# Three of the four weight sums of each pair made by accumulating transfers that GpSimd issues, in place of VectorE additions

## The chip, the cores and the metric

The kernel is one program on one core of a Trainium2 chip. The metric is the time of one execution on the device, in microseconds (us). Engines are named as in the profile: PE is TensorE's matmul side, DVE is VectorE, ACT is ScalarE, POOL is GpSimd, SP is SyncE, which here only issues transfers. A trailing q (SPq) is an engine's sequencer.

## The reference

One transformer block on 512 tokens of width 1024: a feed-forward part, a mixer of two attentions, and a second feed-forward part. Only the feed-forward parts matter here:

```python
def rmsnorm(x, g):
    xf = x.astype(jnp.float32)
    y = xf * lax.rsqrt(jnp.mean(xf * xf, axis=-1, keepdims=True) + RMS_EPS)
    return (y * g.astype(jnp.float32)).astype(x.dtype)

def swiglu(h, w_gate, w_up, w_down):
    return (jax.nn.silu(h @ w_gate) * (h @ w_up)) @ w_down

def reference(x, ...):
    x = x + 0.5 * swiglu(rmsnorm(x, norm_ffn1[l]), w_ffn1_gate[l], w_ffn1_up[l], w_ffn1_down[l])
    x = x + hybrid_mixer(rmsnorm(x, norm_mix[l]), ...)
    x = x + 0.5 * swiglu(rmsnorm(x, norm_ffn2[l]), w_ffn2_gate[l], w_ffn2_up[l], w_ffn2_down[l])
    return rmsnorm(x, norm_final)
```

The width of the feed-forward part is 2816. Everything is float32.

## The kernel before

**Feed-forward blocks.** There are two, both of the class Ffn; I call them block 1 and block 2. The 2816 hidden features are taken in 22 columns of 128. The first 4 are made plainly (`plain`), the other 18 in 9 pairs (`pair`). A pair computes gate (m = 0) and up (m = 1) for two columns with a scheme that needs 7 block products where the plain way needs 8 (the Strassen-Winograd scheme): weights are cut into A11, A12, A21, A22 (first index: which of the two columns; second: which half of the 1024 inputs), the input into B blocks, and the products take A11, A12, A22 and four sums of weights, S1 to S4. Each sum overwrites a weight tile: S1 goes to A21 (A21 + A22), S2 to A11 (A11 + S1), S3 to A21 again (S2 - A22), S4 to A12 (A12 + S2). So S2 needs S1; S3 and S4 need S2.

**Precision.** Each float32 weight block is split into a high half (ACT, line 236, tile sph) and the remainder (DVE, line 237, tile spl), and PE multiplies in three passes (lines 101 to 103, high by high, high by low, low by high). One block product is a step of 12 matmuls of 256 columns. The tiles of halves have 6 buffers each; the weight tiles (aw) have 16, the 8 of one pair twice.

**Order.** `go` walks a list of steps, each with up to five parts: load, sum, halves, products, and what is done with the result. Loads are recorded 12 steps ahead of the products, sums 6, halves 4. Between the steps of a pair stand steps of the down projection (`down`), whose weights come in 512 KB pieces (tile raw, 4 buffers), are split on ACT (line 92, tile whi) and DVE (line 96, wlo), and are multiplied in matmuls of 512 columns. The scheduler of the language then orders each engine's instructions by the times that it reckons with; an engine runs its own in order. All weights are fetched by SP, one after the other in a fixed order (`fetch`); a fetch waits until the tile that it overwrites is free, and all fetches behind it wait too.

**GpSimd** helps in the attention and at the very end; in the feed-forward pairs it does nothing.

The products of a block's first pair overlap with the last down steps of the plain columns.

Of the kernel before, what the change touches and what calls it, by code (L numbers as in the profile page):

```python
# [12 lines left out]
ALU = mybir.AluOpType  # L13
AX = mybir.AxisListType

S = 512
# [13 lines left out]
def block_kernel(ctx: ExitStack, tc: tile.TileContext, A: dict, out: bass.AP):  # L30
# [7 lines left out]
    nc = tc.nc  # L38
# [78 lines left out]
    for k in range(NK):  # L117
        x = xp.tile([128, S], F32, name=f"x{k}")
# [73 lines left out]
    class Ffn:  # L192
# [114 lines left out]
        def pair(self, f):  # L307
# [3 lines left out]
            def loads(m, j):  # L311
                for i in range(2):
                    A[m, i, j] = self.sp.tile([128, 4, 128], F32, name="aw", tag="aw", bufs=16)
                    fetch(A[m, i, j], self.w[m][f + i][:, 4 * j:4 * j + 4])

            def sums(m, name):

                a11, a12, a21, a22 = [A[m, i, j] for i in range(2) for j in range(2)]
                to, x, y, op = {"S1": (a21, a21, a22, ALU.add), "S2": (a11, a21, a11, ALU.add),
                                "S3": (a21, a11, a22, ALU.subtract), "S4": (a12, a11, a12, ALU.add)}[name]  # L320
                with self.behind_lo():
                    nc.vector.tensor_tensor(to, x, y, op)  # L322

            def halves_of(m, name):
                i, j = {"A11": (0, 0), "A12": (0, 1), "S1": (1, 0), "S2": (0, 0), "S3": (1, 0), "S4": (0, 1),
                        "A22": (1, 1)}[name]
                hi = self.sp.tile([128, 4, 128], F32R, name="sph", tag="sph", bufs=6)
                lo = self.sp.tile([128, 4, 128], F32R, name="spl", tag="spl", bufs=6)
                self.halves_of_x(hi, lo, A[m, i, j])
                half[m, name] = hi, lo  # L330

            def run(m, to, a, b, first):
                if first:
                    bank[m, to] = ps.tile([128, S], F32, name="p" + to, tag={"u": "s", "v": "t", "w": "o"}[to],
                                          bufs=2)[:, :HT]
                hi, lo = half.pop((m, a))
                for k, x in enumerate(self.moving(b)):
                    self.in_pair = mm3(bank[m, to], (hi[:, k], lo[:, k]), x, first and k == 0, k == 3, not first)
                    if k == 1:
                        self.between(self.held == 0 and len(self.waiting) > 4)  # L340
                self.between(self.held == 0)
                self.held = max(self.held - 1, 0)

            def copied(m, to, name):
                part[m, name] = self.sp.tile([128, HT], F32, name="wc", tag="wc", bufs=4)
                nc.scalar.activation(part[m, name], bank[m, to], AF.Copy)  # L346
# [29 lines left out]
            for n, (to, a, b, first, then) in enumerate((  # L376
                    ("u", "A11", "B11", True, lambda m: copied(m, "u", "u1")),
                    ("v", "A12", "B21", True, c11),
                    ("w", "S1", "T1", True, lambda m: copied(m, "w", "w1")),
                    ("u", "S2", "T2", False, lambda m: copied(m, "u", "u2")),  # L380
                    ("u", "S3", "T3", False, c22),
                    ("w", "S4", "B22", False, c12),
                    ("u", "A22", "T4", False, c21))):
                for m in range(2):
                    steps.append([(lambda m=m, n=n: loads(m, n)) if n < 2 else None,
                                  (lambda m=m, a=a: sums(m, a)) if a[0] == "S" else None,
                                  lambda m=m, a=a: halves_of(m, a),
                                  lambda m=m, to=to, a=a, b=b, first=first: run(m, to, a, b, first),
                                  lambda m=m, then=then: then(m)])
# [75 lines left out]
        def go(self, after):  # L465
            steps, at = self.steps, [0, 0, 0]
            late, count = None, 0
            for i, s in enumerate(steps):
                for j, ahead in enumerate((12, 6, 4)):
                    while at[j] < min(i + ahead + 1, len(steps)):  # L470
                        if steps[at[j]][j]:
                            steps[at[j]][j]()
                        at[j] += 1
                down = len(s) == 6
                if down and late:
                    late()
                s[3]()
                if not down:
                    if late:
                        late()  # L480
                    if i == 2 * FP - 1:
                        s[4]()
                        s[4] = None
                    after(count)
                    count += 1
                late = s[4]
            if late:
                late()
            self.between(len(self.waiting))
# [757 lines left out]
```

## Time and profile before

| | |
|---|---|
| median of 3 runs | 992.03 us (991.65 to 992.7) |
| profiled execution | 990.21 us, its span 988.4 |
| granted TensorE clock | 0.997 of full speed |
| PE busy | 970.5 us, 98% of the span |
| DVE busy | 778.5 us, 79% |
| ACT busy | 561.9 us, 57% |
| POOL busy | 132.5 us, 13% |
| weight sums on DVE (line 322) | 144 |

How to read the views. A busy time is the union of an engine's instructions. Matmuls are pipelined: a row of one lasts longer than the distance to the next start, so PE can lose a tenth of a microsecond between two matmuls and still be shown busy. In a timeline the square bracket holds the engine's idle time before an instruction and what ended it. A table of stretches gives each engine's busy time in a stretch, the number of instructions, the granted clock, DMA's busy share and the rate that it moved. For transfers, the time from issue to landing is given as a median.

### The profile page before, as it was taken

The page shows a single profiled execution, that of the slowest core. Times are in us where ns is not written, and L with a number is a line of the kernel's source. Part 1 is how long each engine was busy: PE and PEld are TensorE (multiplying, and loading weights), DVE is VectorE, ACT ScalarE, POOL GpSimd, SP SyncE. Part 2 cuts the span into 40 slices and gives each one's busy share as a digit, 9 for nine tenths or more (in the row PEclk, how much of TensorE's full clock was granted, in tenths as well). Part 3 has the DMA queues.
Part 4 walks back from the last instruction along what each step waited for, and adds up shares of the span by engine and source line. Part 5 has one row for each costly group of instructions (what it writes and reads, how often), then busy time and mean ns, then how long its engine had stood idle before and what let it go on. Part 6 is the DMA issues. An engine that isn't in the chain of part 4 may idle for free.

```text
span 988.4 us, 16902 instructions
## 1 busy us (share of the span) xinstructions
PE 970.5 (98%) x6084; PEld 859.0 (87%) x6084; DVE 778.5 (79%) x1579; ACT 561.9 (57%) x1165; POOL 132.5 (13%) x176
## 2 busy tenths in 40 slices
PE   9999999999999999999999999999999999999996
PEld 7789999999999898787878888888999999999985
DVE  6996997688776587768788978789898788777744
ACT  6464655445544366567677886655475445454435
POOL 0000000000000000035666676100000000000002
PEclk9999999999999999999999999999999999999998
DMA  7255534332321125531121232226254322341102
GB/s 257 97 185 173 196 129 133 110 102 91 97 68 43 58 88 190 181 113 33 53 72 43 87 85 80 71 86 213 67 166 153 119 73 95 101 128 44 54 11 86
DMA packets 50056, 104.52 MB, mean 106 GB/s; under 512 B 10129, under 2 KB 14690, under 8 KB 49972
## 3 DMA queue, kind: packets, MB, share of 16 engines
q1 hardware_dynamic: 49684, 102.91, 32.4%
q8 instruction: 48, 0.79, 0.3%
q10 hardware_dynamic: 288, 0.52, 0.1%
q14 instruction: 36, 0.29, 0.1%
HBM read 97.98 MB, written 5.30 MB: 104 GB/s over the span
## 4 chain that ended last, share of the span: by engine, by line
PE 91%; DVE 4%; issue 1%; ACT 1%; DMA 1%; POOL 0%; SPq 0%; POOLq 0%; ACTq 0%; DVEq 0%
PE pd L102 8%; PE pd L103 8%; PE pd L101 8%; PE pu L101 6%; PE pu L103 6%; PE pu L102 6%; PE pw L101 4%; PE pw L103 4%; PE pw L102 4%; PE pp L103 3%; PE pp L101 3%; PE pp L102 3%; PE pgu L102 3%; PE pgu L101 3%; PE pgu L103 3%; PE ps_t L940 3%
## 5 line engine op out<-in xcount | busy, mean ns | idle before, releaser
L236 ACT ACTIVATE sph<-aw 128x512 fp32r<-128x512 f32 x252 | 157.3, 630 | 197.4 <-PE pu L102 71.1
L237 DVE TENSOR_TENSOR spl<-aw,sph 128x512 fp32r<-128x512 f32 x252 | 172.3, 690 | 59.7 <-ACT sph L236 57.2
L92 ACT ACTIVATE whi<-raw 128x512 fp32r<-128x512 f32 (+1 forms) x200 | 121.5, 619 | 126.4 <-PE pd L102 44.2
L102 PE MATMUL pd<-h,whi 128*128 128x512 f32 x336 | 132.7, 395 | 0.0
L103 PE MATMUL pd<-h,wlo 128*128 128x512 f32 x336 | 131.1, 393 | 0.0
L96 DVE TENSOR_TENSOR wlo<-raw,whi 128x512 fp32r<-128x512 f32 (+1 forms) x168 | 111.7, 676 | 24.1 <-ACT whi L92 20.6
L101 PE MATMUL pd<-h,whi 128*128 128x512 f32 x336 | 130.4, 394 | 0.0
L101 PE MATMUL pu<-th,sph 128*128 128x256 f32 x432 | 119.4, 276 | 0.3 <-ACT wc L346 0.3
L103 PE MATMUL pu<-th,spl 128*128 128x256 f32 x432 | 119.4, 276 | 0.0
L102 PE MATMUL pu<-tl,sph 128*128 128x256 f32 x432 | 119.2, 276 | 0.0
L322 DVE TENSOR_TENSOR aw<-aw 128x512 f32<-128x512 f32 x144 | 99.0, 689 | 0.0
L531 DVE SCALAR_TENSOR_TENSOR x<-pd,x 128x512 f32<-128x512 f32 x88 | 60.1, 689 | 33.3 <-PE pd L103 33.3
L101 PEld LDWEIGHTS pu<-th,sph 128*128 128x128 f32 x432 | 81.1, 188 | 4.6 <-ACT wc L346 0.5
L102 PEld LDWEIGHTS pu<-tl,sph 128*128 128x128 f32 x432 | 81.1, 188 | 4.0
L103 PEld LDWEIGHTS pu<-th,spl 128*128 128x128 f32 x432 | 81.1, 188 | 0.1
L101 PE MATMUL pw<-xo,sph 128*128 128x256 f32 x288 | 79.7, 277 | 0.2 <-ACT sph L236 0.2
L102 PE MATMUL pw<-xo,sph 128*128 128x256 f32 x288 | 79.5, 276 | 0.0
L103 PE MATMUL pw<-xo,spl 128*128 128x256 f32 x288 | 79.4, 277 | 0.0
L103 PEld LDWEIGHTS pd<-h,wlo 128*128 128x128 f32 x336 | 63.1, 188 | 13.8
L102 PEld LDWEIGHTS pd<-h,whi 128*128 128x128 f32 x336 | 63.1, 188 | 4.0
L101 PEld LDWEIGHTS pd<-h,whi 128*128 128x128 f32 x336 | 63.1, 188 | 3.7
L101 PEld LDWEIGHTS pw<-xo,sph 128*128 128x128 f32 x288 | 54.1, 188 | 3.9 <-ACT sph L236 0.6
(246 smaller groups left out, 2443.1 us busy)
## 6 DMA issues: line engine op xcount, KB each, us to landing
aw<-in_wg SPq DMA_DIRECT2D x72, 256.0 KB, 2.8
aw<-in_wu SPq DMA_DIRECT2D x72, 256.0 KB, 4.5
raw<-in_wd1a SPq DMA_DIRECT2D x20, 512.0 KB, 3.9
raw<-in_wd2a SPq DMA_DIRECT2D x20, 512.0 KB, 4.8
raw<-in_w_a SPq DMA_DIRECT2D x16, 512.0 KB, 4.8
raw<-in_w SPq DMA_DIRECT2D x8, 512.0 KB, 4.0
raw<-in_w_o SPq DMA_DIRECT2D x8, 512.0 KB, 3.6
raw<-in_wg SPq DMA_DIRECT2D x7, 512.0 KB, 3.6
```

The costliest lines, as they stand in the source:

```text
L92: last_hi[0] = nc.scalar.activation(hi, v, AF.Copy)
L96: nc.vector.tensor_tensor(lo, v, f32(hi), ALU.subtract)
L101: nc.tensor.matmul(p, w[0], v[0], start=first, stop=False, skip_group_check=again)
L102: nc.tensor.matmul(p, w[0], v[1], start=False, stop=False, skip_group_check=again)
L103: return nc.tensor.matmul(p, w[1], v[0], start=False, stop=last, skip_group_check=again)
L236: nc.scalar.activation(hi, v, AF.Copy)
L237: self.last_lo = nc.vector.tensor_tensor(lo, v, f32(hi), ALU.subtract)
L322: nc.vector.tensor_tensor(to, x, y, op)
L531: nc.vector.scalar_tensor_tensor(xs[d], p, 0.5, xs[d], ALU.mult, ALU.add)
L940: nc.tensor.transpose(p[:, wide:wide + 128], lps[qi][:, j * 128:(j + 1) * 128], ident)
```

## The change

Sums S1, S2 and S4 are no longer made on DVE. GpSimd issues a transfer from one weight tile in SBUF to another that adds what it brings to what lies there (`accum_op`). The target must be one of the two addends, so for S2 and S4 the operands are swapped to name it first. S3 is a difference with another target and stays on DVE; it is recorded right behind the halves of S2 instead of at its own place. Sums are recorded 8 steps ahead in place of 6. The lines behind move by 5.

```diff
-                to, x, y, op = {"S1": (a21, a21, a22, ALU.add), "S2": (a11, a21, a11, ALU.add),
-                                "S3": (a21, a11, a22, ALU.subtract), "S4": (a12, a11, a12, ALU.add)}[name]
-                with self.behind_lo():
-                    nc.vector.tensor_tensor(to, x, y, op)
+                to, x, y, op = {"S1": (a21, a21, a22, ALU.add), "S2": (a11, a11, a21, ALU.add),
+                                "S3": (a21, a11, a22, ALU.subtract), "S4": (a12, a12, a11, ALU.add)}[name]
+                if name == "S3":
+                    with self.behind_lo():
+                        nc.vector.tensor_tensor(to, x, y, op)
+                else:
+                    nc.gpsimd.dma_start(to, y, accum_op=op)
...
                 half[m, name] = hi, lo
+                if name == "S2":
+                    sums(m, "S3")
...
-                                  (lambda m=m, a=a: sums(m, a)) if a[0] == "S" else None,
+                                  (lambda m=m, a=a: sums(m, a)) if a in ("S1", "S2", "S4") else None,
...
-                for j, ahead in enumerate((12, 6, 4)):
+                for j, ahead in enumerate((12, 8, 4)):
```

SP's order of transfers is the same before and after. The attention's order is the same on all engines but for line numbers.

On GpSimd there stood nothing between the identity matrix at the start and the attention's first memset; now 54 transfers of block 1 stand there, and 54 of block 2 ahead of the last stage's work. The rows behind the first eight (both sums of S1, S2 and S4 of the first pair and S1 of the second), in block 1. aw_870 and aw_895 hold S1 of the second pair (gate, up), aw_868 and aw_893 S2, aw_918 and aw_941 S4; aw_1165 and aw_1190 are S1 of the third pair:

```order
L325 DMA aw_1165<-aw_1216 128x512
L325 DMA aw_868<-aw_870 128x512
L325 DMA aw_1190<-aw_1239 128x512
L325 DMA aw_893<-aw_895 128x512
L325 DMA aw_918<-aw_868 128x512
L325 DMA aw_941<-aw_893 128x512
```

S1 of a pair thus stands ahead of S2 of the pair before it, on an engine that runs in order.

On DVE, in the second pair of block 1, before (L322 are sums, L237 the low halves, L269 low halves of the hidden features, L350 an addition of results):

```order
L237 TENSOR_TENSOR spl<-aw,sph 128x512
L322 TENSOR_TENSOR aw<-aw 128x512
L269 TENSOR_TENSOR h<-t,h 128x512
L237 TENSOR_TENSOR spl<-aw,sph 128x512
L322 TENSOR_TENSOR aw<-aw 128x512
L350 TENSOR_TENSOR t<-pv,wc 128x256
L237 TENSOR_TENSOR spl<-aw,sph 128x512
L322 TENSOR_TENSOR aw<-aw 128x512
```

and after:

```order
L237 TENSOR_TENSOR spl<-aw,sph 128x512
L323 TENSOR_TENSOR aw<-aw 128x512
L355 TENSOR_TENSOR t<-pv,wc 128x256
L237 TENSOR_TENSOR spl<-aw,sph 128x512
L355 TENSOR_TENSOR t<-pv,wc 128x256
L237 TENSOR_TENSOR spl<-aw,sph 128x512 x5
```

The sums between the halves are gone but for S3.

On PE, where the second pair's S2 of the up part ends (L103 of pu) and S4 begins (pw, with the high half sph_1262 of gate and sph_1280 of up), before:

```order
L103 MATMUL pu_1148<-th3_141,spl_1193 128x256
L101 MATMUL pw_1221<-xo_650,sph_1262 128x256
L102 MATMUL pw_1221<-xo_651,sph_1262 128x256
L101 MATMUL pw_1245<-xo_650,sph_1280 128x256
L102 MATMUL pw_1245<-xo_651,sph_1280 128x256
L101 MATMUL pu_1124<-th3_141,sph_1217 128x256
```

and after:

```order
L103 MATMUL pu_1148<-th3_141,spl_1194 128x256
L101 MATMUL pw_1222<-xo_650,sph_1262 128x256
L102 MATMUL pw_1222<-xo_651,sph_1262 128x256
L103 MATMUL pw_1222<-xo_650,spl_1263 128x256
L101 MATMUL pw_1222<-xo_660,sph_1262 128x256
L102 MATMUL pw_1222<-xo_661,sph_1262 128x256
```

Before, two products of each S4 stood ahead of S3's; now all 12 of gate's S4 and then 4 of up's do.

## Rows read from the trace of the kernel before

**Rows 1.** The page, busy time, share and instructions of each engine.
```profile
PE 970.5 (98%) x6084; PEld 859.0 (87%) x6084; DVE 778.5 (79%) x1579; ACT 561.9 (57%) x1165; POOL 132.5 (13%) x176
```
**Rows 2.** Stretches: us, busy PE, PEld, DVE, ACT, POOL, clock, DMA share, GB/s.
```profile
50.00:150.00 100.00, 99.52 (x707) 92.38 (x706) 89.59 (x164) 58.40 (x118) 0.00 (x0) 1.00 0.49 167
150.00:330.00 180.00, 180.00 (x1267) 166.25 (x1266) 134.59 (x235) 84.83 (x164) 0.00 (x0) 1.00 0.30 91
690.00:750.00 60.00, 59.78 (x460) 57.03 (x460) 52.94 (x96) 33.02 (x66) 0.00 (x0) 1.00 0.32 106
750.00:950.00 200.00, 200.00 (x1415) 185.01 (x1414) 154.50 (x270) 96.78 (x189) 0.00 (x0) 1.00 0.28 92
```
**Rows 3.** PE's timeline at 108 us: start, duration, instruction, idle time before it.
```profile
108.10 0.28 PE L101 MATMUL pw<-xo,sph 128*128 128x256 f32 x1
108.21 0.28 PE L102 MATMUL pw<-xo,sph 128*128 128x256 f32 x1
...
109.47 0.39 PE L101 MATMUL pu<-th,sph 128*128 128x256 f32 x1 [0.29 <-ACT wc L346]
109.70 0.28 PE L102 MATMUL pu<-tl,sph 128*128 128x256 f32 x1
```
**Rows 4.** PE's timeline at 98, 734 and 743 us.
```profile
98.41 0.28 PE L102 MATMUL pv<-xo,sph 128*128 128x256 f32 x1
...
98.87 0.28 PE L102 MATMUL pw<-xo,sph 128*128 128x256 f32 x1
...
733.98 0.28 PE L101 MATMUL pw<-xo,sph 128*128 128x256 f32 x1
...
743.38 0.28 PE L102 MATMUL pv<-xo,sph 128*128 128x256 f32 x1
...
744.10 0.28 PE L102 MATMUL pu<-xo,sph 128*128 128x256 f32 x1
```
**Rows 5.** Sums on DVE: in all (busy us, mean ns, idle before); from 97 to 113 us.
```profile
L322 DVE TENSOR_TENSOR aw<-aw 128x512 f32<-128x512 f32 x144 | 99.0, 689 | 0.0
...
L322 DVE TENSOR_TENSOR aw<-aw 128x512 f32<-128x512 f32 x6 | 4.1, 688 | 0.0
```
**Rows 6.** ACT's timeline: two splits of raw pieces.
```profile
96.40 1.16 ACT L92 ACTIVATE whi<-raw 128x512 fp32r<-128x512 f32 x2 [2.37 <-DMA raw<-in_wd1a]
...
742.92 0.64 ACT L92 ACTIVATE whi<-raw 128x512 fp32r<-128x512 f32 x1 [2.74 <-DMA raw<-in_wd2a]
```
**Rows 7.** SP's timeline: start and duration of issues, two merged into a row at x2.
```profile
86.19 1.46 SPq L66 DMA_DIRECT2D aw<-in_wg  x2
88.94 1.69 SPq L66 DMA_DIRECT2D aw<-in_wu  x2
90.68 0.42 SPq L66 DMA_DIRECT2D raw<-in_wd1a  x1
...
715.10 1.69 SPq L66 DMA_DIRECT2D aw<-in_wu  x2
```
**Rows 8.** GpSimd's own subtractions of a tile, in the attention: busy us, mean ns, idle.
```profile
L94 POOL TENSOR_TENSOR wlo<-raw,whi 128x512 fp32r<-128x512 f32 x32 | 42.3, 1322 | 12.3 <-ACT whi L92 10.0 <-PE ps_t L940 2.2
```
**Rows 9.** A transfer from SBUF to SBUF: count, KB each, median us to landing.
```profile
ak<-ak SPq DMA_DIRECT2D x16, 128.0 KB, 2.2
```
**Rows 10.** Transfers from 80 to 120 us: count, KB each, median us to landing.
```profile
aw<-in_wu SPq DMA_DIRECT2D x8, 256.0 KB, 5.4
raw<-in_wd1a SPq DMA_DIRECT2D x4, 512.0 KB, 6.6
aw<-in_wg SPq DMA_DIRECT2D x7, 256.0 KB, 4.4
```
**Rows 11.** Loads of weight tiles (aw) from 150 to 330 us.
```profile
DMA to landing us min/median/max: 2.4/3.4/4.0
```
**Rows 12.** Stretches of 10 us, columns as in rows 2.
```profile
90.00:100.00 10.00, 10.00 (x88) 9.84 (x87) 7.20 (x15) 5.82 (x11) 0.00 (x0) 1.00 0.81 268
100.00:110.00 10.00, 9.52 (x81) 9.12 (x81) 10.00 (x20) 8.11 (x18) 0.00 (x0) 1.00 0.21 63
```

## The prediction

> **What bounds the kernel now.** I read the page first for the shares of the engines. PE is busy 970.5 of 988.4 us [rows 1], so what the change can give must lie in the 18 us in which PE is idle, or in stalls that the modelled ends of matmuls cover. The second view is the table of stretches, for the stages that the change touches, the pair stages of the two feed-forward blocks. From 150 to 330 us and from 750 to 950 us PE is busy in every microsecond, and DVE only 134.59 of 180 and 154.50 of 200 [rows 2]. There a shorter DVE buys nothing. The idle time is in the first pairs of a block: 0.48 us in the 100 us from 50, 0.22 in the 60 from 690 [rows 2]. I call these first three pairs the ramp.
>
> A matmul row lasts longer than the distance to the next start, so the third view is PE's timeline there, read by starts. Nothing waiting, a product of 256 columns starts 0.113 us after the one before (108.10, 108.21 in [rows 3]). From 108.21 to 109.70 four steps take 1.49 us instead of 0.45: a stall of 1.04 us [rows 3]. Two more are found the same way: from 98.41 to 98.87 two steps take 0.46 instead of 0.23, from 743.38 to 744.10 two take 0.72 [rows 4], stalls of 0.23 and 0.49. These 1.04 + 0.23 + 0.49 = 1.76 us are all that I find PE to lose in the pair stages.
>
> Fourth, who ended them. Before 108 DVE runs without a pause; between 97 and 113 us it makes 6 sums, 4.1 us, with no idle time before them [rows 5], so the stall of 1.04 is DVE's backlog. The other two have another cause: ACT stood 2.37 us until 96.40 and 2.74 us until 742.92 for a raw piece of the down weights [rows 6]; the halves queued behind it on ACT come late.
>
> **What is removed.** Of the 144 sums at 689 ns [rows 5], 36 in each of 4 names, 108 leave DVE: 108 x 0.689 = 74.4 us. S3's 36 stay. On PE's path lies only the backlog, so I count **-1.04 us**, once; the second block has no such stall. The other 73 us of DVE lie beside PE and become idle time.
>
> **What is added, and its price.** 108 transfers on GpSimd's queue, each of which reads 2 x 256 KB and writes 256 KB. GpSimd has no work in either pair stage, so its time to issue them is hidden; I call it g, and take 1 us, between the 0.42 that an issue takes on SP [rows 7] and the 1.32 of GpSimd's own operation on a tile of this size [rows 8]. What counts is L, from GpSimd's turn (g included) until the sum has landed. No row shows an accumulating transfer. From below: a copy from SBUF to SBUF of half the size lands in 2.2 us [rows 9]. From above: 512 KB from HBM, as much as an accumulation reads, lands in 6.6 us in the ramp, with g of 1.3 that makes 7.9; 256 KB takes 4.4 to 5.4 there [rows 10], and 2.4 to 4.0 once the ramp is over [rows 11]. I take L = 5, nearest to the 256 KB rows plus g, since the size per partition is theirs; a cost below nothing is excluded, as each sum waits for its transfer. The Trainium skill ("DMA: Bandwidth & Descriptors", section "Anatomy of one DMA — SWDGE (gpsimd) path") gives a fixed 2.0 us plus the bytes at 436 GB/s; for 256 KB that is an estimate of 2.6 us, for 512 KB 3.2. By it the ramp chain below would have two microseconds to spare in each link and the first rival would fall away; the loads of this trace take longer than that in the ramp [rows 10], and the sum goes by them.
>
> **Steady part: nothing.** A pair takes PE about 30 us: 14 steps of 12 products of 0.113, and 4 fill steps of 12 with 512 columns, at twice that. So the 18 steps take 1.66 each. On GpSimd S2 of a pair stands behind S1 of the next pair. That next pair's last load waits until the halves of the previous pair's last A22 are made, four steps ahead of its products, that is about 12 of 18 steps, 20 us, into the previous pair. With 4.0 for the load [rows 11] and g, S2 starts 25 us into a pair of 30, or 5 ahead of its own; S4 lands at -5 + 2L, and PE comes to it after 8 steps and some 2 fills, at +17, less 1.3 for the halves. That holds up to L = 10, so the term is 0 for all of the bounds.
>
> **Ramp: the chain S1, S2, S4.** Here the same order on GpSimd is tight. In block 1 the last A22 load of the third pair is the second of the two issues that begin at 88.94 [rows 7], at about 90.3; with 5.4 us [rows 10] it lands at 95.7. GpSimd issues S1 of that pair, and only then S2 of the second pair's up part: from 96.7, landed at 96.7 + L, and S4 at 96.7 + 2L. PE came to the gate part's S4 at 108.10 [rows 3]; in the new order all 12 of its products stand there before the up part's first, 12 x 0.113 = 1.36 later, at 109.46. ACT's 0.64 and DVE's 0.69 for the halves (one operation of that size in [rows 5, 6]) must fit in before, so S4 must have landed by 108.1. That gives 2L <= 11.4, L <= 5.7. In block 2 the load is issued at 715.10 + 1.4 [rows 7], lands at about 721.9 with the same 5.4, so S2 begins at 722.9; PE came to S4 at 733.98 [rows 4], now 735.34 for the up part, 734.0 less the halves: L <= 5.6. With L = 5 both hold by a little over 1 us: **0**. The traffic helps, since DMA's share falls from 0.81 to 0.21 at 100 us [rows 12], when S4 is moved. Every microsecond of L beyond costs 2 us in each block.
>
> **Ramp: the raw pieces.** They have no slack at all, as both stalls show. In block 1 the piece is issued at 90.68 [rows 7] and lands just before 96.40. Between 91.7 (the gate part's A22 load, second of the two issues from 86.19 [rows 7], at 87.3 + 4.4 [rows 10]) and then, S1 of the third pair and S2 of the second are moved. The stretch moves 268 GB/s at a share of 0.81 [rows 12], 331 GB/s at a full one, so 256 KB cost 0.79 us of all engines, and an accumulation one to three times that. Two of them delay the piece by 0 (they come behind it) to 4.8 us (all ahead); I take half of two accumulations at 1.25 times 0.79, nearer to the lower end since the piece is issued first, and PE pays it one for one: **+1.0 us**. In block 2 one accumulation falls into the piece's flight (bounds 0 to 2.4): **+0.5**. The Trainium skill ("DMA: Bandwidth & Descriptors", "Issuing engines are not separate DMA queues") speaks against the change here: transfers of GpSimd and SP run on the same 16 engines and interleave. If they did not, both terms would be 0 and the time that of the second rival; the up part's loads, 5.4 us in the busy ramp against at most 4.0 later [rows 10, 11], agree with the rule.
>
> **Sum.** -1.04 + 1.0 + 0.5 + 0 = +0.5 us on the profiled execution of 990.21 (span 988.4 and 1.8 around it): 990.7. The median of the runs, 992.03, stands 1.82 above that execution: **992.5 us**. A measurement here can tell about 0.2% from no change, 2.0 us; this is within it.
>
> **Rivals.**
> 1. The ramp chain is late (slower). Its place is the second pair's S4, its point L = 5.7. For it: L is unseen, its upper bound is 7.9, and the share before 100 us is 0.81 [rows 12]. Against it: S4 travels in a quiet stretch. At L = 7 it costs 2 x 1.3 + 2 x 1.4 = 5.4 us: 998. At L = 6.5 it is 3.4, 996. Up to 6.0 the sum stays within the 0.2%.
> 2. The raw pieces are not delayed and only the backlog goes: 992.03 - 1.04 = 991.0. Even with all 1.76 us of stalls gone it is 990.3, 0.18%, so still within. For it: the pieces are issued ahead of the accumulations. Against it: they are still in flight when these start.
> 3. L is over 10: the steady part waits as well. Each microsecond over costs 2 us in each of some 14 pairs after the ramp, so L = 12 gives 56 us, some 1050. For it speaks only that the operation is unseen; against it, no weights of up to 512 KB have a median over 6.6 us [rows 10].
>
> Faster by over 0.2% would take more than every stall that the rows show, so something that they don't show.
>
> **How the numbers follow.** The forecast has 0.58, the first rival 0.24, the second 0.09, the third 0.05, something faster 0.04. Same is 0.58 + 0.09 = 0.67; slower 0.24 + 0.05 = 0.29; faster 0.04. The range begins at 990.2, where all stalls are gone, and ends at 998, the first rival at L = 7; what lies outside is the third rival, the upper third of the first and most of faster, about 0.16.
>
> **What would show it.** In the changed kernel's profile: 36 sums on DVE and some 704 us of DVE busy time; PE without idle time from 150 to 330 and from 750 to 950; no stall at 108 that ends with DVE; ACT's wait for the raw piece near 96 and 743 longer by half to one microsecond, and PE's stall with it; the accumulations landing in about 5 us. The first rival would show as PE or ACT waiting for a transfer into the weight tiles around 105 to 112 and 731 to 737 us; the third as that wait in every pair. I am wrong at the root if PE's products of 256 columns no longer start 0.113 us apart, or if the transfers are issued in another order.

## The result: 0.66% slower, and the profile after

| | before | after |
|---|---|---|
| median of the runs | 991.84 us (991.48 to 992.70) | 998.37 us (997.49 to 999.78) |
| ratio | | 1.0066, 95% interval 1.0048 to 1.0083 |
| profiled execution, its span | 990.21, 988.4 us | 998.74, 996.8 us |

The forecast was 992.5 us, within 0.2% of before, with a range to 998.0. The time came out 0.4 us above that range. The two profiled executions lie 8.4 us of span apart and the medians 6.5: the profiled one of before was a quick one. The first line of the page after, to be read beside [rows 1]:

```profile
PE 975.1 (98%) x6084; PEld 863.5 (87%) x6084; DVE 723.3 (73%) x1471; ACT 564.4 (57%) x1165; POOL 227.4 (23%) x284
```

The stretches of [rows 2] after the change (block 2 begins some 5 us later now), columns us, busy PE, PEld, DVE, ACT, POOL, clock, DMA share, GB/s:

```profile
50.00:150.00 100.00, 96.89 (x671) 90.06 (x670) 74.01 (x136) 55.50 (x112) 20.71 (x24) 0.98 0.85 227
150.00:330.00 180.00, 180.00 (x1270) 166.40 (x1269) 119.32 (x204) 86.24 (x166) 26.70 (x31) 1.00 0.57 136
690.00:750.00 60.00, 57.95 (x408) 54.31 (x407) 43.02 (x79) 31.01 (x61) 12.75 (x15) 0.97 0.71 174
750.00:950.00 200.00, 200.00 (x1434) 185.88 (x1433) 138.49 (x237) 100.94 (x195) 32.74 (x38) 1.00 0.60 146
```

The steady part is as forecast: PE is busy in all of its 180 and 200 us. The loss is in the two ramps. PE's clock, 1.00 in each of these stretches before, is 0.98 and 0.97 there. PE's timeline at the two large stalls (start, duration, instruction, idle time before it and what ended it):

```profile
123.11 0.38 PE L101 MATMUL pu<-xo,sph 128*128 128x256 f32 x1 [2.38 <-ACT t L373]
...
124.17 0.41 PE L101 MATMUL pu<-xo,sph 128*128 128x256 f32 x1
124.38 0.41 PE L102 MATMUL pu<-xo,sph 128*128 128x256 f32 x1
...
733.30 0.38 PE L101 MATMUL pw<-xo,sph 128*128 128x256 f32 x1 [2.05 <-ACT sph L236]
```

Each of the two stalls ends with ACT, and some products later PE runs at half speed: at 124.17 the starts lie 0.21 apart, not 0.113. Stretches around the stalls show the granted clock (last columns: clock, DMA share, GB/s; the share is a sum of packets' recorded times, which can overlap, so it can pass 1):

```profile
118.00:123.00 5.00, 2.74 (x24) 2.53 (x22) 1.05 (x2) 0.84 (x3) 2.65 (x3) 1.00 1.05 410
123.00:128.00 5.00, 4.89 (x28) 4.89 (x29) 2.32 (x4) 1.62 (x4) 0.86 (x1) 0.66 1.08 238
128.00:133.00 5.00, 5.00 (x40) 4.73 (x39) 3.28 (x6) 2.87 (x7) 1.76 (x2) 1.00 0.70 123
733.00:738.00 5.00, 4.70 (x26) 4.62 (x27) 4.72 (x9) 4.03 (x9) 1.17 (x2) 0.66 0.66 119
```

Counted by the distances of starts, as the prediction did it, the ramp of block 1 loses 1.5 us up to 116, 2.65 at the stall of 123 and 1.6 in 15 products at half speed: 5.8, against 1.3 before. Block 2 loses 2.4 at the stall of 733 and 1.7 at half speed: 4.1, against 0.5. The differences, 4.5 and 3.6, are 8.1 of the 8.4 us.

What had ACT waited for? Its timeline in the ramps:

```profile
96.30 1.16 ACT L92 ACTIVATE whi<-raw 128x512 fp32r<-128x512 f32 x2 [2.21 <-DMA raw<-in_wd1a]
...
103.85 1.15 ACT L92 ACTIVATE whi<-raw 128x512 fp32r<-128x512 f32 x2 [2.11 <-DMA raw<-in_wd1a]
...
122.16 0.63 ACT L92 ACTIVATE whi<-raw 128x512 fp32r<-128x512 f32 x1 [4.71 <-DMA raw<-in_wd1a]
122.69 0.37 ACT L373 ACTIVATE t<-pu 128x256 f32<-128x256 f32 x1
...
731.58 1.15 ACT L92 ACTIVATE whi<-raw 128x512 fp32r<-128x512 f32 x2 [2.54 <-DMA raw<-in_wd2a]
```

Both times ACT stood for a raw piece of the down weights, and behind it in ACT's order stood what PE needed next. The half that is split at 122.16 is multiplied first some 40 us later, so nobody was in a hurry for it. It was not the piece at 96 that came late, as forecast: that one is there at 96.30, as before [rows 6].

The piece of 122.16 was not slower in flight. From its issue to its split it took 6.8 us, before 6.7 (113.14 to 119.79). It was issued 2.2 us later, because SP stood ahead of a weight load. SP before, then after:

```profile
106.46 1.19 SPq L66 DMA_DIRECT2D aw<-in_wg  x2
...
113.14 0.33 SPq L66 DMA_DIRECT2D raw<-in_wd1a  x1
```

```profile
106.53 3.49 SPq L66 DMA_DIRECT2D aw<-in_wg  x2
...
115.37 0.49 SPq L66 DMA_DIRECT2D raw<-in_wd1a  x1
```

The second load of the row at 106.53 was issued at 109.69. The trace has SP waiting there for the semaphore of the second pair's last S4 transfer, which landed at 109.55. The piece of 731.58 is another case: issued at 722.54 in time, it took 9.0 us beside three transfers issued from 722 to 725; before, it took at most 5.7 (717.31 to 723.02).

Last, GpSimd's issues in the ramp of block 1, and the time from issue to landing of all 108 transfers and then of those from 80 to 136 us alone:

```profile
91.16 1.76 POOL L325 DMA_DIRECT2D aw<-aw  x2 [17.03 <-DMA aw<-in_wu]
94.63 0.86 POOL L325 DMA_DIRECT2D aw<-aw  x1 [1.70 <-DMA aw<-in_wu]
99.90 0.88 POOL L325 DMA_DIRECT2D aw<-aw  x1 [4.41 <-DVE t L376]
101.64 0.87 POOL L325 DMA_DIRECT2D aw<-aw  x1 [0.86 <-DVE h L269]
105.71 0.86 POOL L325 DMA_DIRECT2D aw<-aw  x1 [3.20 <-issue]
119.42 2.65 POOL L325 DMA_DIRECT2D aw<-aw  x3 [12.85 <-DVE spl L237]
```

```profile
DMA to landing us min/median/max: 3.3/4.3/9.0
DMA to landing us min/median/max: 3.5/5.9/9.0
```

The median of 4.3 is close to the forecast's L of 5. But in the ramp, where three transfers fly beside weight loads and raw pieces, they take up to 9.0. And GpSimd stands for 12.85 us before 119.42: the S1 of the fourth pair waits there for that pair's weights, and the S2 of the third pair stands behind it.

Two theories came out of this: the raw pieces hold up ACT, or the chain of sums is late (the prediction's first rival).

### The profile page after: what moved, and what is told of

The parts are those of the page before. It is cut to its first block, busy times and chain, and to the rows that moved or that the text cites. A ratio compares the mean times of both kernels' runs of the same rounds, so it can differ in the third digit from the quotient of the medians.

```text
span 996.8 us, 17114 instructions
## 1 busy us (share of the span) xinstructions
PE 975.1 (98%) x6084; PEld 863.5 (87%) x6084; DVE 723.3 (73%) x1471; ACT 564.4 (57%) x1165; POOL 227.4 (23%) x284
## 3 DMA queue, kind: packets, MB, share of 16 engines
q1 hardware_dynamic: 49684, 102.91, 32.1%
q0 software_dynamic: 15552, 28.32, 16.9%
## 4 chain that ended last, share of the span: by engine, by line
PE 90%; DMA 3%; DVE 3%; issue 1%; ACT 1%; POOL 0%; SPq 0%; POOLq 0%; DVEq 0%; ACTq 0%
PE pd L102 8%; PE pd L103 8%; PE pd L101 8%; PE pu L101 6%; PE pu L103 6%; PE pu L102 6%; PE pw L101 4%; PE pw L103 4%; PE pw L102 4%; PE pp L103 3%; PE pp L101 3%; PE pp L102 3%; PE pgu L101 3%; PE pgu L102 3%; PE pgu L103 3%; PE ps_t L945 3%
## 5 line engine op out<-in xcount | busy, mean ns | idle before, releaser
L237 DVE TENSOR_TENSOR spl<-aw,sph 128x512 fp32r<-128x512 f32 x252 | 172.8, 690 | 103.1 <-ACT sph L236 98.0
L325 POOL DMA_DIRECT2D aw<-aw x108 | 94.7, 948 | 496.8 <-DMA aw<-in_wg 153.4
L103 PE MATMUL pd<-h,wlo 128*128 128x512 f32 x336 | 131.1, 393 | 0.0
L103 PE MATMUL pu<-th,spl 128*128 128x256 f32 x432 | 119.5, 277 | 0.0
L103 PEld LDWEIGHTS pu<-th,spl 128*128 128x128 f32 x432 | 81.1, 188 | 0.1
L103 PE MATMUL pw<-xo,spl 128*128 128x256 f32 x288 | 79.9, 277 | 0.3 <-DVE spl L237 0.3
L103 PEld LDWEIGHTS pd<-h,wlo 128*128 128x128 f32 x336 | 63.1, 188 | 13.8
```

Of the source, the lines that this page charges most:

```text
L103: return nc.tensor.matmul(p, w[1], v[0], start=False, stop=last, skip_group_check=again)
L237: self.last_lo = nc.vector.tensor_tensor(lo, v, f32(hi), ALU.subtract)
L325: nc.gpsimd.dma_start(to, y, accum_op=op)
```

## The experiments

Ratios are against the kernel before, run on the same chip, with 95% intervals.

### Where: the ramp alone

**The first three pairs keep their sums on DVE** (`by_dma` is new; such pairs take the old branch, six steps ahead).

```diff
+            by_dma = f >= FP + 6
...
-                if name == "S3":
+                if name == "S3" or not by_dma:
```

> The first three pairs of each block keep all their sums on DVE, six steps ahead, as before the change; the other twelve pairs use the transfers. Theory A (all of the loss lies in the two ramps: pieces of the down weights land late beside the transfers, ACT stands for them, PE with it, and its clock falls to half for some microseconds): 991 to 993 us, PE without idle time from 150 to 330 and 760 to 960, no stretch at half clock near 123 or 733. Theory B (the transfers cost PE something in every pair, which the rows don't show): two thirds of the loss stay, 996 to 997.

Measured: 990.76 us, 0.9991 (0.9981 to 1.0001). The 72 transfers of the other twelve pairs cost nothing.

**The counterpart**, `by_dma = f < FP + 6`.

> The counterpart: only the first three pairs of each block use the transfers, the other twelve sum on DVE. Theory A: the whole loss stays, 997 to 999 us, with the stalls of over 2 us on PE near 123 and 733 and half clock behind them. Theory B: a third of the loss, 993.5 to 994.5.

Measured: 1006.21 us, 1.0139 (1.0119 to 1.0159). The loss is in the ramp, but it is twice as large as with all transfers, which neither theory had. ACT and PE there:

```profile
125.79 0.63 ACT L92 ACTIVATE whi<-raw 128x512 fp32r<-128x512 f32 x1 [9.40 <-DMA raw<-in_wd1a]
```

```profile
127.26 0.58 PE L101 MATMUL pu<-xo,sph 128*128 128x256 f32 x1 [6.95 <-ACT t L375]
```

The fourth pair has no transfers here, so nothing holds the third pair's S2 back on GpSimd: it is issued at 114.39, not 120.02, and flies beside the very piece that ACT waits for. That piece, issued at 115.80, takes 10.0 us until its split instead of 6.8. Transfers that come earlier are no better.

### What: relief, bytes, the addition

**S1, S2 and S4 left out.**

```diff
-                    nc.gpsimd.dma_start(to, y, accum_op=op)
+                    pass
```

> S1, S2 and S4 are not made at all: neither DVE nor a transfer touches them, their products use the weight tiles as they were loaded. What is left of the change is the relief of DVE. Theory A: 990.3 to 991.3 us, the time of before less the stalls of 1.04 to 1.76 us. A rival by which a shorter DVE queue or the new order of PE costs by itself: 994 or more.

Measured: 992.11 us, 0.9995 (0.9978 to 1.0013). Even with nothing in place of the sums, DVE's relief is worth nothing. The stall of [rows 3] at 108 is gone, but another takes its place (ACT, then PE):

```profile
118.41 0.63 ACT L92 ACTIVATE whi<-raw 128x512 fp32r<-128x512 f32 x1 [4.05 <-DMA raw<-in_wd1a]
```

```profile
119.88 0.39 PE L101 MATMUL pu<-xo,sph 128*128 128x256 f32 x1 [1.42 <-ACT t L373]
```

The reason is ACT's order, which the scheduler makes anew for each kernel. Before, the instruction that PE waits for (t<-pu, line 368) stood ahead of this split; since the change it stands behind it, as the rows at 122 showed. Before:

```profile
116.14 0.39 ACT L368 ACTIVATE t<-pu 128x256 f32<-128x256 f32 x1 [0.79 <-PE pu L103]
116.42 0.62 ACT L236 ACTIVATE sph<-aw 128x512 fp32r<-128x512 f32 x1
119.79 0.64 ACT L92 ACTIVATE whi<-raw 128x512 fp32r<-128x512 f32 x1 [2.75 <-DMA raw<-in_wd1a]
```

**Half of each transfer** (the other half of a sum is left out).

```diff
-                    nc.gpsimd.dma_start(to, y, accum_op=op)
+                    nc.gpsimd.dma_start(to[:, :2], y[:, :2], accum_op=op)
```

> Each accumulating transfer adds only half of the tile (two of its four blocks of 128 columns); the other half of each sum is left out. Their number, their places and their waits stay. Theory S (what they cost is their time on the shared DMA engines, by bytes): DMA's share from 150 to 330 falls from 0.58 to about 0.44, the pieces are late by half as much, 992 to 994.5 us. Rival: the cost is per transfer, not per byte (issue, fixed part): the share stays near 0.58, 997 or more.

Measured: 992.48 us, 1.0008 (0.9996 to 1.0020).

**The same transfers without the addition**, plain copies.

```diff
-                    nc.gpsimd.dma_start(to, y, accum_op=op)
+                    nc.gpsimd.dma_start(to, y)
```

> The same 108 transfers without the addition, plain copies from tile to tile (the sums S1, S2 and S4 are left out). It prices the accumulation by itself. From 150 to 330 us the accumulating transfers raise DMA's share by 0.28 over 180 us for 30 of them, 1.7 us of all engines each, twice what a load of 256 KB takes there (0.9). If the addition is the dear part, copies cost 0.9 or less, the share is about 0.44, and the time 992 to 994.5; if any transfer from SBUF to SBUF costs this much, 0.58 and 997 or more.

Measured: 992.78 us, 1.0010 (0.9999 to 1.0021). The stretch from 150 to 330 us with half transfers, then with copies:

```profile
150.00:330.00 180.00, 180.00 (x1267) 166.22 (x1266) 119.48 (x205) 85.47 (x164) 24.61 (x28) 1.00 0.46 111
```

```profile
150.00:330.00 180.00, 180.00 (x1266) 166.24 (x1265) 119.93 (x205) 85.36 (x165) 15.10 (x28) 1.00 0.43 132
```

DMA's share is 0.30 before [rows 2], 0.57 after the change, 0.46 with halves, 0.43 with copies. The addition thus doubles the time on the shared DMA engines: the added share is 0.13 for copies and 0.27 for accumulations. That the loss goes with this time fits both runs but is not shown by them, since their transfers also land earlier and set the rest of the chain free earlier. Both runs keep a stall on a raw piece near 120, like the run without sums.

### Which wait: the pieces or the chain

**The pieces fetched earlier** (down steps get a counter of their own, 16 steps ahead).

```diff
-                for j, ahead in enumerate((12, 8, 4)):
+                for q, j, ahead in ((3, 0, 16), (0, 0, 12), (1, 1, 8), (2, 2, 4)):
...
```

> The changed kernel with one edit: the pieces of the down weights that are multiplied between the pairs are fetched 16 steps ahead instead of 12, so ahead of some weight tiles in SP's order. Theory A, late pieces: ACT no longer waits 4.7 us until 122 nor 2.5 until 731, both stretches at half clock vanish, 991 to 994 us. Theory D (the chain S1, S2, S4 makes ACT and PE late, the pieces only come last by chance): the stalls move to a wait for a weight tile, 997 us or more, since the weight tiles are now fetched later.

Measured: 1003.09 us, 1.0100 (1.0075 to 1.0124). A miss for both theories: in the profiled execution, the quickest of four by 3 us, the two large stalls moved to 101.7 (3.2 us) and 746 (2.9 us), and they still stand behind ACT's wait for a raw piece, not for a weight tile. The scheduler put the splits earlier on ACT as well, so an earlier fetch gave them no more time.

**One weight tile more.**

```diff
-name="aw", tag="aw", bufs=16)
+name="aw", tag="aw", bufs=17)
```

> The changed kernel with 17 weight tiles (aw) in place of 16. A fetch then overwrites a tile that was given up one load earlier, so SP stands less behind the transfers that still read or write the tile. Theory Q (in block 1 the third piece of the down weights is late because it is issued 2.3 us later, behind a weight load that waits for the transfer of S4): the stall near 123 and the half clock behind it shrink by 2 to 4 us, 994 to 996.5. Theory S (the pieces are late only because the transfers share the DMA engines with them): 998 as before this edit, or more.

Measured: 998.01 us, 1.0058 (1.0039 to 1.0077). Inconclusive: single runs lie between 994.4 and 999.4, and the profiled one is the quickest of them. In it the third piece is issued at 112.60 and PE's stall behind it is 1.1 us in place of 2.65, as theory Q has it; the median is that of theory S.

**A piece fetched twice, in the kernel before.**

```diff
                     fetch(raw[d * n // 8], w[d * n // 8])
+                    if fs[0] == FP and d == 4:
+                        fetch(raw[d * n // 8], w[d * n // 8])
```

> The kernel before, all sums on DVE and no transfer of the change. In each block one piece of the down weights, the third of those between the pairs (the one that ACT splits at 119.8 and 742.9), is fetched twice, so it lands about 6 us later. Theory A (a piece that lands late stops ACT, then PE, and PE resumes at half clock): a stall of 3 to 5 us and 1.5 to 2 us of lost clock in each block, 1000 to 1005 us. Rival: ACT and PE have other work to go on with, so a late piece alone costs less than 1 us per block: 991 to 993.

Measured: 990.92 us, 0.9989 (0.9975 to 1.0002): nothing. ACT stood 3.94 us until 123.51 for the piece, longer than before, and PE did not stand there, since the scheduler had moved the split behind three more operations that PE needed. So theory A fell as it was put: a late piece need not cost anything. It costs something where what PE needs next stands behind it.

**The splits pinned on ACT**: a piece's split is queued behind the halves of the pair that are recorded before it. After the change, then before it.

```diff
-            nc.scalar.activation(hi, v, AF.Copy)
+            self.last_of_pair = nc.scalar.activation(hi, v, AF.Copy)
...
-                    with self.behind_lo() if kept_back else nullcontext():
+                    with (self.behind_lo() if kept_back else nullcontext()), (
+                            tc.issue_after(self.last_of_pair.ins) if kept_back else nullcontext()):
```

> The changed kernel with one edit to ACT's order alone: the split of a piece of the down weights (whi) between the pairs is queued behind the halves of the pair that are recorded before it, instead of 10 to 20 us ahead of need. All 108 transfers stay. Theory A2 (the loss is ACT standing in order for a piece that nobody needs yet; the transfers only make it land late): no wait for a piece on ACT of over 1 us near 122 and 731, no half clock behind, 991.5 to 994 us; what remains are the stalls of some 1.9 us from 106 to 112, where PE waits for the chain S1, S2, S4. Theory A1 (late pieces cost this wherever ACT splits them) or the chain as the main cause: 996 or more.

> The same edit to ACT's order in the kernel before, without any transfer of the change. Theory A2: only the stalls of 0.23 and 0.49 us that end behind a piece go, 990.8 to 991.6, the same as before within 0.2%. If the edit by itself were worth several us, it would show here, and the run before would not speak of the transfers.

Measured: after the change 1000.11 us, 1.0078 (1.0064 to 1.0092); in the kernel before 988.93 us, 0.9972 (0.9961 to 0.9984). With the change, no wait for a piece is left, and the loss is still there. Now ACT waits for the sums:

```profile
101.42 0.63 ACT L236 ACTIVATE sph<-aw 128x512 fp32r<-128x512 f32 x1 [3.81 <-DMA aw<-aw]
105.28 0.63 ACT L236 ACTIVATE sph<-aw 128x512 fp32r<-128x512 f32 x1 [3.23 <-DMA aw<-aw]
...
129.03 0.63 ACT L236 ACTIVATE sph<-aw 128x512 fp32r<-128x512 f32 x1 [8.87 <-DMA aw<-aw]
```

So theory A2 fell too: the wait for the pieces had covered the wait for the chain, which runs beside it. The sum behind the wait of 8.87 us is the S2 of the third pair, issued at 120.39, behind the S1 of the fourth.

In the kernel before, the same edit takes away every stall in the ramps, that of [rows 3] included, though DVE makes all the sums:

```profile
50.00:150.00 100.00, 100.00 (x716) 93.39 (x715) 90.90 (x167) 58.02 (x116) 0.00 (x0) 1.00 0.51 167
...
690.00:750.00 60.00, 60.00 (x463) 57.33 (x462) 53.29 (x96) 32.41 (x63) 0.00 (x0) 1.00 0.34 106
```

It is the quickest kernel of the study, 0.28% below before, with all sums on DVE, and below the expected 990.8. The interval, 1.6 to 3.9 us, holds the prediction's 1.76 us of stalls. So the stall of [rows 3] was no load of sums that DVE could not carry. Before, DVE stood 1.91 us for a high half that ACT made behind the raw piece of 96.40, and then ran without a pause, late by that much. With the splits pinned the wait is gone, and DVE is through 1.9 us earlier. DVE before, then in this run:

```profile
98.11 0.69 DVE L237 TENSOR_TENSOR spl<-aw,sph 128x512 fp32r<-128x512 f32 x1 [1.91 <-ACT sph L236]
```

```profile
96.21 0.69 DVE L237 TENSOR_TENSOR spl<-aw,sph 128x512 fp32r<-128x512 f32 x1
```

**Six steps ahead instead of eight.**

```diff
-                for j, ahead in enumerate((12, 8, 4)):
+                for j, ahead in enumerate((12, 6, 4)):
```

> The changed kernel with its transfers recorded six steps ahead, as the sums were before, instead of eight. Theory A2: the transfers still meet the pieces, and the chain S1, S2, S4 has less time, so 998 or more, with a wait of PE for S4 from 106 to 112 of 1 us more than with eight. Rival (the transfers are merely issued too early, into the pieces' flight): 992 to 995.

Measured: 998.15 us, 1.0062 (1.0044 to 1.0080). The two steps are worth nothing either way.

**The second pair on DVE**, `by_dma = f != FP + 2`.

> The changed kernel, but the second pair of each block keeps its four sums on DVE, six steps ahead; the other sixteen pairs use the transfers. The chain S1, S2, S4 whose limit the prediction worked out is then cut, and of the six transfers from 91 to 106 us two remain, the S1 of the third pair. If that chain is the cause: 991 to 993. If the pieces' lateness is, through all that is in flight with them: block 1 still loses 1 to 3 us near 120, since the weights of the fourth pair and the S1 of that pair are there too: 993 to 996.

Measured: 995.77 us, 1.0041 (1.0028 to 1.0053). Some two fifths of the loss go with the one pair for which the prediction had worked out the chain. What is left are stalls of up to 1.1 us from 98 to 111, one of 0.8 at 134 and 2.1 us in block 2, and PE no longer falls to half speed.

### Both orders at once

**GpSimd's transfers in recorded order**: S1, S2, S4 of a pair, then S1 of the next.

```diff
-                    nc.gpsimd.dma_start(to, y, accum_op=op)
+                    with tc.issue_after(self.last_sum.ins) if self.last_sum else nullcontext():
+                        self.last_sum = nc.gpsimd.dma_start(to, y, accum_op=op)
```

> The changed kernel with GpSimd's transfers in the order in which they are recorded: S1, S2, S4 of a pair, gate and up, and only then S1 of the next pair. Nothing else is edited. Theory P (S2 is late because it stands behind the next pair's S1): the stalls from 106 to 112 and near 730 shrink, 991.5 to 994.5; the wait of ACT for the pieces may stay. Theory L (any transfer is late in the crowded ramp, whatever the order): 997 or more.

> Both edits: GpSimd's transfers in recorded order and ACT's splits of the pieces pinned behind the halves. Theory P: neither the sums nor the pieces are late for anyone, PE has no stall of over 0.5 us in either ramp, 988.5 to 991, as the kernel before with pinned splits (988.9). Theory L: waits of ACT for aw remain at 100 to 112 and 125 to 135, 996 or more.

Measured: the order alone 999.05 us, 1.0085 (1.0062 to 1.0108); with the splits pinned 991.05 us, 0.9991 (0.9980 to 1.0003). With the order alone, the S2 of the third pair is issued at 112.83 and the chain is in time, but now it flies beside the raw piece, and ACT stands for that:

```profile
123.17 0.63 ACT L92 ACTIVATE whi<-raw 128x512 fp32r<-128x512 f32 x1 [7.23 <-DMA raw<-in_wd1a]
```

With both edits, the landing times from 80 to 136 us are no better than after the change:

```profile
DMA to landing us min/median/max: 3.3/7.8/9.1
```

And yet PE stands for long only once in the ramps:

```profile
131.55 0.39 PE L101 MATMUL pu<-th,sph 128*128 128x256 f32 x1 [1.15 <-ACT wc L353]
```

The four corners, as ratios to before:

| | splits as scheduled | splits pinned |
|---|---|---|
| transfers as scheduled | 1.0066 | 1.0078 |
| transfers in recorded order | 1.0085 | 0.9991 |

Either edit alone gains nothing, both together give back the loss against before. Theory P's time is met but for 0.05 us, not its bound of 0.5 us on the stalls. Against the kernel before with the same pinning, 0.9972, some 0.2% is still lost, at the edge of what the two intervals can tell apart. Theories P and L each saw a part: in the ramp transfers take up to 9 us to land whatever the order, and most of what that costs comes through two orders, each of which is enough by itself. On ACT, halves stand behind a piece that nobody needs yet; on GpSimd, the S2 that is needed stands behind an S1 that can't start yet. The longer of two waits that run side by side sets PE's time, so removing one need not show. The total hides a difference, though: counted by starts, block 1 loses some 9.7 us with the splits pinned and 8.9 with the order alone, against 5.8, but block 2 only 1.8 and 0.8, against 4.1. In block 2 either edit helps, and in block 1 each lays bare a longer wait. These are single traces.

### The queue's limit

Why was the S2 of the second pair's up part issued only at 99.90? The transfers' own records show it. In no run are more than three accumulating transfers of 128 rows in flight, and again and again a fourth is issued 0.31 us after the oldest has landed (11 times in the run with both edits). At 99.90 in the timeline of GpSimd above it is so: the time to landing of the transfer of 91.16 is

```profile
DMA to landing us min/median/max: 8.4/8.4/8.4
```

so it landed at 99.6, and the S2 of the second pair's up part, which had been next since 95.5, was issued at 99.90. The profile's own entry there, DVE, is the event that was nearest in time. Of copies, four flew at once. Half tiles met the same limit, but the oldest landed at 97.3, and this S2 followed 0.3 us later:

```profile
97.63 0.88 POOL L325 DMA_DIRECT2D aw<-aw  x1 [1.80 <-issue]
```

Two more runs:

**Half of the rows** (64 of the 128 partitions; the other half of a sum is left out).

```diff
-                    nc.gpsimd.dma_start(to, y, accum_op=op)
+                    nc.gpsimd.dma_start(to[:64], y[:64], accum_op=op)
```

> Each accumulating transfer adds only 64 of the 128 partitions (the other half of each sum is left out): half the bytes, as in the run with half tiles, but half the rows as well. If the limit of three in flight goes by rows, more than three fly at once in the ramp and the second pair's S2 of the up part is issued near 95 instead of after a landing: 991 to 992.5 us. If it goes by the number of transfers, never more than three fly, and the time is that of half tiles, 992.5.

Measured: 993.56 us, 1.0018 (1.0007 to 1.0029). Four flew at once, and that S2 was issued right behind the third, at 95.6, the second in this row:

```profile
95.05 1.65 POOL L325 DMA_DIRECT2D aw<-aw  x2 [1.75 <-DMA aw<-in_wu]
```

So the limit doesn't go by the number of transfers alone, nor by bytes alone: half tiles bring as few bytes as half rows and never flew more than three. The time is over the expected 992.5: a stall of 2.1 us behind the raw piece of 120.62 stays, and one of 0.7 at 99.6.

**S1 on DVE**, so that it neither stands ahead of S2 on GpSimd nor takes up a place.

```diff
-                                  (lambda m=m, a=a: sums(m, a)) if a in ("S1", "S2", "S4") else None,
+                                  (lambda m=m, a=a: sums(m, a)) if a in ("S2", "S4") else None,
...
+                    if a == "S1":
+                        self.on_dve[id(steps[-1])] = lambda m=m, a=a: sums(m, a)
```

> S1 stays on DVE, six steps ahead and ahead of S2, in all pairs; S2 and S4 are transfers (72). If the chain is late because of what S1 takes of GpSimd's queue (its place ahead of S2, its share of the three in flight): ACT waits for aw under 1 us each from 99 to 112, no stall of over 1 us near 130, 991 to 994 us; a stall behind a piece near 120 may stay. If the transfers' traffic and the pieces' place on ACT are enough by themselves: 996 or more.

Measured: 995.08 us, 1.0032 (1.0020 to 1.0045). The chain passes: no wait of ACT for a sum is longer than 0.36 us from 99 to 135. What is left is one raw piece, a stall of 3.2 us on PE and 1.7 us at half speed behind it:

```profile
120.21 0.63 ACT L92 ACTIVATE whi<-raw 128x512 fp32r<-128x512 f32 x1 [5.53 <-DMA raw<-in_wd1a]
```

That is 1.1 us above the range, as the price of the piece was set too low. (A first version, in which S1 stood behind S2 in the program, so that S2 took A21 without A22, ran 1002.80 us and tells nothing of this.)

What stays open: what the limit of three counts, and what it costs by itself. With half the bytes, three in flight ran 1.0008 and four 1.0018, so lifting it gained nothing there.

## Why the prediction was wrong, point by point

- **The bound and the steady part** held: PE sets the end, and twelve pairs with transfers cost nothing (the run with the ramps on DVE, 990.76).
- **What is removed.** DVE's busy time fell by 55.2 us, not 74.4. Rows of DVE at full load start 0.60 us apart though each lasts 0.69, so the sum of durations counted overlaps, 0.09 us at either end: 108 x 0.18 = 19.4, against the 19.2 that are missing. It made no difference for the time.
- **The backlog, -1.04.** The cause was misread. DVE ran without a pause from 98.11 to 108, but it had stood 1.91 us before that, behind the raw piece of 96.40: all three stalls of before begin with a piece in ACT's order, and pinning the splits removed them with the sums still on DVE. The stall of [rows 3] did go after the change, but the relief was not a gain: with nothing in place of the sums the time is 0.9995 of before, since a stall of 1.4 us at 119.88 takes its place, behind a raw piece in ACT's new order.
- **g and L.** g was 0.87 (taken: 1). L has a median of 4.3 (taken: 5), but 5.9 in the ramp and up to 9.0, above even the upper bound of 7.9. One L for a quiet and a crowded stretch was the first mis-sized term. The bound came from a load of 512 KB that shared the DMA engines with other loads, not with two more transfers of the new kind.
- **The ramp chain, taken at 0: the step that failed.** The prediction started the S2 of the second pair at 96.7, right behind S1. S1 was issued at 94.63, earlier than forecast, but S2 only at 99.90, when the oldest of three transfers had landed. The working had a place in the order for it, but no limit to what flies at once. It landed at 105.1, S4 was issued at 105.71 and landed at 109.5, 1.4 us behind the limit of 108.1 that the prediction had worked out, and PE stood in the steps of 106 and 109.7. That is 1.5 us up to 116, little more than the 1.3 of before. The dearer way was SP: its fetches stand in one order, one of them waited for this S4, and so the third raw piece was issued 2.2 us late; behind that piece stand 4.25 of the 5.8 us that block 1 loses. The prediction took SP's order as unchanged and did not ask when its fetches come free. The same chain in the third pair was not worked out at all. It is tighter, as S2 stands behind an S1 whose weights arrive some 14 us after GpSimd's previous issue; this is the wait of 8.87 us that the pinned run laid bare.
- **The raw pieces, +1.0 and +0.5, the other term that failed.** In the changed kernel the two large stalls stand behind pieces and cost, with the clock, 4.25 and 4.1 us. Place and size were wrong, the mechanism was right in part. The first piece was not delayed. Slower in flight were the second of block 1 (issued at 92.77, split at 103.85, 11.1 us; before 7.8) and the second of block 2; the third of block 1 was late by its issue, see above. The prediction took an accumulation at 1.25 times a load's time on the engines; the queues' totals of the page after give about twice:

```profile
q1 hardware_dynamic: 49684, 102.91, 32.1%
q0 software_dynamic: 15552, 28.32, 16.9%
```

  Columns are packets, MB and share of 16 engines' span. 16.9% of 996.8 us over 108 transfers is 1.56 us of all engines each; SP's loads take 32.1% for 102.91 MB, 0.82 us per 256 KB. The forecast's 0.79 times 1.25 is 0.99.
- **The Trainium skill's figure** ("DMA: Bandwidth & Descriptors", "Anatomy of one DMA — SWDGE (gpsimd) path"), by which 256 KB would take an estimated 2.6 us, is below every transfer of this trace, which take 3.3 at least; the trace decides. The other rule weighed there ("Issuing engines are not separate DMA queues") is borne out: the second piece of block 1 took 11.1 us with three of GpSimd's transfers in flight, 7.8 without.
- **Not counted at all:** the clock. After each of the two large stalls PE ran 15 products at half speed, 1.6 and 1.7 us, two thirds as much again as the stalls of 2.65 and 2.4.
- **The rivals.** The first, the chain, was the likeliest of the wrong cases and named the right mechanism, with 996 to 998 us; its price by the formula (two blocks, L at most 7.9) left out the third pair, the fetches and the clock. That its time came so near to the measured one is luck. The chance of 0.24 for it rested on the quiet DMA share of 0.21 from 100 to 110 us before [rows 12]; after the change it is 0.86, as the moved transfers were themselves traffic there.

## What to carry to other kernels

Work that is moved from an engine to DMA is free only where its landing time is covered, and that has to be asked separately for the crowded stretches, with everything that will fly there, the moved transfers included. Read the order behind each new wait on every engine that runs in order: a transfer that can't start yet, ahead of one that is needed, and a split of data that nobody needs yet, ahead of data that PE needs, each can cost a whole landing time. So can a fetch that waits for a tile in use by a transfer, ahead of all the fetches behind it. Where taking away one wait changes nothing, look for a second one beside it before dropping the theory; here the total time showed either only when both were gone.

## What the runs showed of the hardware that was not expected

- An accumulating transfer of 256 KB from SBUF to SBUF, issued by GpSimd, held GpSimd for 0.87 us and landed in 3.3 us at the least, 4.3 in the median, and in 7 to 10 where three flew beside weight loads (10.0 in the run with pinned splits). On the DMA engines it cost about twice a load of the same size (1.56 against 0.82 us of all 16). A plain copy held GpSimd for 0.54 us (15.10 us for 28 in the stretch above).
- No more than three accumulating transfers of 128 rows were ever in flight from GpSimd; a fourth was issued 0.31 us after a landing. Four of 64 rows were, and four plain copies. By an estimate from the 7 to 9 us that each takes in the ramp, GpSimd gets out at most some three in 8 us there.
- The granted clock fell to half (the lower of TensorE's levels, 1.2 GHz) soon after work had come back from the stalls of 2.38 and 2.05 us, for some 3 us. At the stalls of 6.95 us in the run with only the ramps on transfers and of 4.59 with GpSimd's order alone it fell while PE still stood, and stayed down for some 7 us. It stayed at 1.00 after the stall of 1.42 in the run without sums. The first of the long ones, PE at rest and then at work again (columns as in the tables of stretches, the clock before the last two):

```profile
124.50:127.20 2.70, 0.00 (x0) 0.00 (x0) 0.23 (x1) 1.41 (x4) 0.82 (x1) 0.50 1.07 382
127.20:131.20 4.00, 3.94 (x18) 3.94 (x19) 4.00 (x8) 2.99 (x7) 0.00 (x0) 0.50 0.80 175
```
